# Hybrid decoder layer in three FFN passes: what stands between two passes, and the order of convolution and norm at the mixers' end

## The chip, the cores and the metric

The kernel runs on one core of a Trainium2 chip. The metric is the device time of one execution in microseconds (us); smaller is better. TensorE (PE) does the matmuls and transposes, VectorE (DVE) elementwise work and reductions, ScalarE (ACT) activations and some copies, GpSimd (POOL) a few small powers, and SyncE (SP) issues nearly all DMAs. Each engine runs its own instructions strictly in the order in which they stand in its program; engines wait for one another by semaphores.

## What is computed

One decoder layer and the final norm, for 2048 prompt tokens and 8 x 4 sample tokens, all in float32 (model width 1024, FFN width 2816):

```
xn   = rmsnorm(h) ; proj = xn @ w_in                  # q, f, i, og | ca, cg
o_a  = HGRN2 recurrence on 4 heads, normed, * silu(og)
o_b  = silu(layernorm(conv31(ca * sigmoid(cg))))      # depthwise, 31 taps
h    = h + concat(o_a, o_b) @ w_out                   # h1
xn2  = rmsnorm(h)
h    = h + (silu(xn2 @ w_gate) * (xn2 @ w_up)) @ w_down      # h2
gate = sigmoid(rmsnorm(h) @ w_ple_gate)
h    = h + gate * (p @ w_ple_proj)                    # h3, p: embedding inputs
y    = rmsnorm(h) * g_final
```

## The kernel before

**Precision.** A float32 product is made of three matmuls on a high and a low part of each operand (`mm3`, lines 541 to 544; in the FFN `mm3s`, line 1632): low x high, high x high, high x low. One weight tile pair `wh`, `wl` (128x512 each) serves four steps of the inner dimension, 12 matmuls.

**Order.** Python generators ("threads") yield operations, waits for events and requests for buffers. A list scheduler (`Sched.run`) with its own clocks picks, at build time, the next operation of each engine: the earliest possible start, and between equals the lower `pen` given at `spawn`. For a TensorE operation of a side thread that could not start at once by its clocks, it adds `SIDE` ns to that start, so that matmuls go ahead of it. What it picks is the fixed program order on the chip.

**Stages.** The mixers run over 8 blocks of 256 tokens, the last one with the 32 sample tokens: in-projection, heads, convolution on DVE (line 393, penalties `PCV` 400 and `PCL` 300), layernorm (`bn` lines 942 to 974), out-projection with the residual input `x_in`. Its result h1 is written to DRAM (`h1d`) and also read back from there. Then come three FFN passes t = 0, 1, 2 over 2 x 348, 2 x 348 and 2 x 344 tokens (two halves h). In a pass the gate and up products are made Strassen-like: seven products over 2x2 blocks (A12, A11, S1, S2, S4, S3, A22; `strassen`), each over four steps kp = 0 to 3 of the inner dimension. Weight pairs for passes 1 and 2 are read from `tch`, `tcl` into a ring of nine.

**What stands around the change.** `norm2(t)` makes the FFN's RMS factor `r2[h]` for both halves and then starts `combine(t, kp)` for kp = 0 to 3: it loads four pieces of h1 (DMA, tiles `h` and `f`), scales each by norm gain and r2 (SCALAR_TENSOR_TENSOR, `gn,r`), and makes the seven operands by sums and high/low splits (`x2h`, `x2l`, `xah`, `xal`). Each combine needs five `tmp2` buffers. `residual()` loads h1 into the tiles to which the down-projection adds. `embed(t)` is the per-layer embedding step at the end of a pass; `norm3(t, h)` is its norm, which gives `r3[h]`; its inputs p are loaded by `pin_load` and fire `pin`. `norm4(t, h)` is the final norm: squares on ACT, adds on DVE, then in `rms2` three transposes on TensorE (line 1315), two reductions (lines 1319, 1322), a power on POOL (line 426), three transposes that spread the factor (line 1330), and eight SCALAR_TENSOR_TENSORs (`gn,px`), each followed by `store_y`.

In the kernel before, `norm2(t)` for t > 0 lets the combines begin only after these waits:

```
yield wait(("a", t - 1, last_chunk, CHUNKS[-1] - 1, 1))
for k in range(2):
    for h in HALVES:
        yield wait(("pin", t - 1, k, h))
for h in HALVES:
    yield wait(("r3", t - 1, h))
```

Of the kernel before, what the change touches and what calls it, by code (L numbers as in the profile page):

```python
# [60 lines left out]
NEARA = 80  # L61
NEARD = 40
PSQ = 0
RANK = {"o": -2.0}
FIRST = "ca0 cg0 iv f0 q0 ca1 cg1 f1 q1 ca2 cg2 f2 q2 ca3 cg3 f3 q3 og"

# [29 lines left out]
class Sched:  # L96
# [2 lines left out]


    LAT = 200.0
    SIDE = 1000.0
    OWN = 130.0
    near = dict(pe=0.0, act=NEARA, dve=NEARD, pool=60.0, sp=0.0)

# [82 lines left out]
    def run(self, last=True):  # L188
        self.advance()
        while self.ready:  # L190
            best = {}
            for i, (th, req) in enumerate(self.ready):
                s = self.start(req)
                e = req[1]
                if e == "pe" and th[0].__name__ not in ("lane", "ffn") and s > self.clock[e]:

                    s += self.SIDE
                rank = (th[3] if th[0].__name__ in ("lane", "ffn") else -9.0) if e == "pe" else th[1]
                key = (max(s, self.clock[e] + self.near[e]), rank, th[2])
                if e not in best or key < best[e][0]:  # L200
                    best[e] = (key, s, i)
            _, s, i = min(best.values(), key=lambda x: x[1])
            th, req = self.ready.pop(i)
            _, eng, dur, fn, R, W, nbytes = req
            fn()
            if eng == "sp":
                self.clock["sp"] = s + 60.0
                self.dma = max(self.dma, s) + nbytes / RATE
                end = self.dma + 2000.0
            else:  # L210
                end = s + dur
                self.clock[eng] = end
            for b in R:
                b.r = max(b.r, end)
            for b in W:
                b.w = end
                b.we = eng
            self.runnable.append((th, None))
            self.advance()
        if last and (self.blocked or any(p.waiting for p in self.pools)):  # L220
            said = [f"{th[0].__name__} waits for {ev}" for ev, ths in self.blocked.items() for th in ths]
            said += [f"{th[0].__name__} waits for {n} of {p.name}" for p in self.pools for th, n in p.waiting]
            raise RuntimeError("stuck:\n" + "\n".join(said))
# [19 lines left out]
def trunk(ctx: ExitStack, tc: tile.TileContext, x_in, p_in, s0_in, c0_in, w_in, w_out, w_gu, w_dn,  # L243
# [1021 lines left out]

    def residual():
        for t in PASSES:
            for m in range(KD):
                for h in HALVES:
                    q = yield acq(hres)  # L1270
                    yield from h1_load(t, h, m, q)
                    res[t, m, h] = q
                    S.fire(("hr", t, m, h))
# [10 lines left out]
            sq[k] = q  # L1284
            S.fire(("sq", tag, k))

    def rms2(n, get):

        tk = toks(n)
        tag, sq = count[0], {}  # L1290
        count[0] += 1
        S.spawn(squares2(n, get, sq, tag), PSQ)
        acc = [None, None]
        for i in range(KD):
            yield wait(("sq", tag, i))
            if i < 2:
                acc[i] = sq[i]
                continue
            a, q = acc[i % 2], sq[i]
            if i == 2:  # L1300
                yield stt(a.ap[:, 0:n], a.ap[:, 0:n], EPS / 128, q.ap[:, 0:n], ALU.add, ALU.add, R=[a, q], W=[a], n=n)
            else:
                yield tt(a.ap[:, 0:n], a.ap[:, 0:n], q.ap[:, 0:n], ALU.add, R=[a, q], W=[a], n=n)
            S.release(tmp2, q)
        a, q = acc
        yield tt(a.ap[:, 0:n], a.ap[:, 0:n], q.ap[:, 0:n], ALU.add, R=[a, q], W=[a], n=n)
        S.release(tmp2, q)
        ss = yield acq(small)
        tn = tk[-1][1]
        yield op("dve", 80.0, lambda: nc.vector.memset(ss.ap[:, 2:3], 1.0), [], [ss])  # L1310
        bank = yield acq(misc)

        def fn():
            for j, (t, w) in enumerate(tk):
                nc.tensor.transpose(bank.ap[0:w, j * 128:(j + 1) * 128], a.ap[:, t:t + w], idn)

        yield op("pe", 100.0 * len(tk), fn, R=[a], W=[bank])
        S.release(tmp2, a)
        yield op("dve", d_tt(256), lambda: nc.vector.tensor_reduce(
            out=ss.ap[:, 0:2], in_=bank.ap[:, 0:256].rearrange("p (j f) -> p j f", j=2),  # L1320
            axis=mybir.AxisListType.X, op=ALU.add), [bank], [ss])
        yield op("dve", d_tt(128), lambda: nc.vector.tensor_reduce(  # L1322
            out=ss.ap[0:tn, 2:3], in_=bank.ap[0:tn, 256:384], axis=mybir.AxisListType.X, op=ALU.add), [bank], [ss])
        S.release(misc, bank)
        yield inverse_root(ss, 128, 0, 8, 3)
        bank = yield acq(misc)

        def fn():
            for j, (t, w) in enumerate(tk):
                nc.tensor.transpose(bank.ap[:, t:t + w], ss.ap[0:w, 8 + j:9 + j].to_broadcast([w, 128]), idn[0:w, 0:w])  # L1330

        yield op("pe", 100.0 * len(tk), fn, R=[ss], W=[bank])
        S.release(small, ss)
        return bank
# [7 lines left out]
    def norm2(t):  # L1342
        if t:
            yield wait(("a", t - 1, 2, 1, 1))
        for h in HALVES:
            def get(k, h=h):
                q = yield acq(tmp2)
                yield from h1_load(t, h, k, q)
                return q, q

            yield from row(HALF[t], get, r2[h], ("r2", t, h))
        if t:
            yield wait(("a", t - 1, last_chunk, CHUNKS[-1] - 1, 1))
            for k in range(2):
                for h in HALVES:
                    yield wait(("pin", t - 1, k, h))
            for h in HALVES:
                yield wait(("r3", t - 1, h))
        else:
            yield wait(("indone", NBLK - 2))  # L1360
            yield wait(("indone", NBLK - 1))
        for kp in range(KP):
            if t == 0 and kp == 2:
                yield wait("ffn")
            if t and kp:

                yield wait(("x2", t, kp - 1, "S3"))
            five = yield acq(tmp2, 5)
            S.spawn(combine(t, kp, five), 350 if t == 0 and kp < 2 else 150 if t else 0)

    def combine(t, kp, five):
        n = HALF[t]
# [51 lines left out]
    S.spawn(lane(1), 30)  # L1424
    S.spawn(load_states(), 0)
    S.spawn(free_tmp2(), 0)
    S.spawn(norm2(0), 350)
    manual = tc.manual_schedule()
    manual.__enter__()
    S.run(False)  # L1430
# [528 lines left out]

    def norm4(t, h):  # L1960
        n = HALF[t]
        bank = yield from rms2(n, of_res(t, h, "h3"))
        for m in range(KD):
            r = res[t, m, h]
            ra = r.ap[:, 0:n]
            yield stt(ra, ra, gn[:, 3, m:m + 1], bank.ap[:, 0:n], ALU.mult, ALU.mult, R=[r, bank], W=[r], n=n)
            S.spawn(store_y(t, h, m), 0)
        S.release(misc, bank)
# [132 lines left out]
```

## Time and profile before

| | us |
|---|---|
| runs | 2639.54, 2645.95, 2644.22 (median 2644.22) |
| profiled execution | 2645.72 |
| its span in the trace | 2644.0 |
| TensorE busy | 2525.0 (96%) |
| VectorE busy | 1978.4 (75%) |
| ScalarE busy | 1082.1 (41%) |
| mean granted TensorE clock | 0.98 of full |

TensorE is busy nearly all the time, so what is to be gained or lost is mostly in the few stretches where it is not. Between neighbouring matmuls of 348 columns the starts lie 0.16 us apart at full clock and 0.29 us at the lower level; a matmul is listed with 0.32 or 0.49 us, since neighbours overlap in the pipeline. In a row of the timeline, the bracket at the end gives the idle time of the engine before that row and what ended it.

### The profile page before, as it was taken

The numbers are of one execution on the slowest core, as the hardware profiler recorded it, in microseconds if no ns is written. First come the engines' busy times: TensorE is split into PE (matmuls) and PEld (weight loads), VectorE is DVE, ScalarE is ACT, GpSimd is POOL, SyncE is SP. The second block draws the span as 40 slices with busy tenths as digits, with TensorE's granted clock in tenths as the row PEclk, the third lists the DMA queues.
The fourth block names the chain that finished last, engine by engine and source line by source line (L and its number), as shares of the span: only waits on it lengthen the run. The fifth ranks groups of instructions, "written<-read, shape, count | busy, mean of one in ns | idle before, by whom it ended". The sixth has DMA issues, their size and how long they took to land.

```text
span 2644.0 us, 44170 instructions
## 1 busy us (share of the span) xinstructions
PE 2525.0 (96%) x15646; PEld 2368.0 (90%) x15646; DVE 1978.4 (75%) x4578; ACT 1082.1 (41%) x2477; POOL 140.4 (5%) x286
## 2 busy tenths in 40 slices
PE   7999999999999799999999899999998799999988
PEld 6987977778887699999999889999998799999977
DVE  8998899679886876666677857686587666677686
ACT  5553344334332343444354433343344334333353
POOL 0111010010110100000000000000000000000010
PEclk9999999999999799999999999999999899999999
DMA  8665646554546684565452374445622555554433
GB/s 310 222 211 187 236 159 199 197 179 162 165 139 204 201 278 164 187 211 177 159 207 74 128 255 169 154 161 192 216 81 96 163 193 195 196 173 162 148 95 118
DMA packets 290510, 470.86 MB, mean 178 GB/s; under 512 B 46576, under 2 KB 88048, under 8 KB 290288
## 3 DMA queue, kind: packets, MB, share of 16 engines
q1 hardware_dynamic: 287984, 466.63, 52.7%
q8 instruction: 123, 2.02, 0.3%
q10 hardware_dynamic: 2304, 1.41, 0.2%
q14 instruction: 99, 0.81, 0.1%
HBM read 368.27 MB, written 99.64 MB: 177 GB/s over the span
## 4 chain that ended last, share of the span: by engine, by line
PE 87%; DVE 6%; DMA 3%; POOL 1%; ACT 1%; issue 1%; SPq 0%; POOLq 0%; DVEq 0%; ACTq 0%
PE pm L1632 27%; PE px L1632 13%; PE pm L542 11%; PE pm L544 11%; PE pm L543 11%; PE px L544 2%; PE px L542 2%; PE px L543 2%; DVE h L390 1%; DVE wl L390 1%; PE pm L610 1%; PE pm L612 1%; PE pm L611 1%; DVE h L393 1%; POOL sm L426 1%
## 5 line engine op out<-in xcount | busy, mean ns | idle before, releaser
L390 DVE TENSOR_TENSOR wl<-raw,wh 128x512 fp32r<-128x512 f32 (+1 forms) x496 | 328.8, 667 | 151.8 <-ACT wh L385 138.9
L385 ACT ACTIVATE wh<-raw 128x512 fp32r<-128x512 f32 (+1 forms) x496 | 295.9, 608 | 309.4 <-PE pm L543 96.5
L542 PE MATMUL pm<-xal,wh 128*128 128x256 f32 (+2 forms) x960 | 324.0, 337 | 8.8 <-DVE xal L390 4.6
L544 PE MATMUL pm<-xah,wl 128*128 128x256 f32 (+2 forms) x960 | 311.1, 324 | 0.9 <-DMA wl<-wcl 0.9
L543 PE MATMUL pm<-xah,wh 128*128 128x256 f32 (+2 forms) x960 | 310.9, 324 | 0.0
L542 PE MATMUL pm<-xol,wh 128*128 128x348 f32 (+4 forms) x751 | 250.7, 334 | 9.2 <-ACT wh L385 5.2
L544 PE MATMUL pm<-xoh,wl 128*128 128x348 f32 (+4 forms) x751 | 246.4, 328 | 0.6 <-DVE wl L390 0.5
L543 PE MATMUL pm<-xoh,wh 128*128 128x348 f32 (+4 forms) x751 | 246.1, 328 | 0.0
L390 DVE TENSOR_TENSOR h<-pm,h 128x348 f32<-128x348 f32 (+1 forms) x335 | 172.5, 517 | 91.5 <-PE pm L544 42.6
L1632 PE MATMUL pm<-xal,wh 128*128 128x348 f32 (+1 forms) x707 | 228.6, 323 | 4.1 <-DVE h L390 1.8
L1632 PE MATMUL pm<-xah,wh 128*128 128x348 f32 (+1 forms) x707 | 227.6, 322 | 0.0
L1632 PE MATMUL pm<-xah,wl 128*128 128x348 f32 (+1 forms) x707 | 227.4, 322 | 0.1
L542 PEld LDWEIGHTS pm<-xal,wh 128*128 128x128 f32 x960 | 183.1, 191 | 36.0 <-issue 8.6
L393 DVE SCALAR_TENSOR_TENSOR t<-u,cvw,t 128x256 f32<-128x256 f32 x448 | 214.0, 478 | 0.0
L544 PEld LDWEIGHTS pm<-xah,wl 128*128 128x128 f32 x960 | 182.3, 190 | 15.8 <-DMA wl<-wcl 1.8
L385 ACT ACTIVATE wh<-tw 128x512 fp32r<-128x512 f32 x146 | 92.0, 630 | 249.7 <-DVE tw L390 92.9
L543 PEld LDWEIGHTS pm<-xah,wh 128*128 128x128 f32 x960 | 183.0, 191 | 11.7
L1632 PE MATMUL pm<-x2l,wh 128*128 128x348 f32 (+1 forms) x533 | 171.5, 322 | 6.1 <-DVE x2l L390 6.1
L426 POOL TENSOR_TENSOR sm<-sm,mhalf 128x2 f32<-128x2 f32 (+3 forms) x79 | 75.1, 952 | 1851.7 <-DVE sm L1322 1736.7
L393 DVE SCALAR_TENSOR_TENSOR h<-u,cvw,h 128x256 f32<-128x256 f32 x360 | 171.1, 476 | 2.2 <-ACT h L385 2.1
L1632 PE MATMUL pm<-x2h,wh 128*128 128x348 f32 (+1 forms) x533 | 171.7, 322 | 0.0
L1632 PE MATMUL pm<-x2h,wl 128*128 128x348 f32 (+1 forms) x533 | 171.7, 322 | 0.0
(292 smaller groups left out, 6513.7 us busy)
## 6 DMA issues: line engine op xcount, KB each, us to landing
raw<-w_gu SPq DMA_DIRECT2D x220, 256.0 KB, 3.2
wh<-wch SPq DMA_DIRECT2D x192, 256.0 KB, 2.8
wl<-wcl SPq DMA_DIRECT2D x192, 256.0 KB, 3.2
wh<-tch SPq DMA_DIRECT2D x176, 256.0 KB, 4.6
wl<-tcl SPq DMA_DIRECT2D x176, 256.0 KB, 4.8
raw<-w_dn SPq DMA_DIRECT2D x132, 256.0 KB, 3.2
tch<-wh SPq DMA_DIRECT2D x88, 256.0 KB, 2.8
tcl<-wl SPq DMA_DIRECT2D x88, 256.0 KB, 2.9
```

What stands on the lines that cost most here:

```text
L385: nc.scalar.activation(out, in_, func, scale=scale, bias=bias, **kw)
L390: return op("dve", d_tt(n), lambda: nc.vector.tensor_tensor(out=out, in0=a, in1=b, op=o), R, W)
L393: return op("dve", d_tt(n, not isinstance(s, float)), lambda: nc.vector.scalar_tensor_tensor(out=out, in0=a, scalar=s, in1=b, op0=o0, op1= ...
L426: return op("pool", 700.0, lambda: nc.gpsimd.tensor_tensor(out=s.ap[0:rows, out:out + n], in0=s.ap[0:rows, lo:lo + n], in1=mhalf[0:rows, 0 ...
L542: nc.tensor.matmul(out, lhsT=wh, rhs=xl, start=first, stop=False)
L543: nc.tensor.matmul(out, lhsT=wh, rhs=xh, start=False, stop=False)
L544: nc.tensor.matmul(out, lhsT=wl, rhs=xh, start=False, stop=last)
L610: nc.tensor.matmul(bank.ap, lhsT=xs[0], rhs=wl, start=(k == 0), stop=False)
L611: nc.tensor.matmul(bank.ap, lhsT=xs[0], rhs=wh, start=False, stop=False)
L612: nc.tensor.matmul(bank.ap, lhsT=xs[1], rhs=wh, start=False, stop=(k == KD - 1))
L1632: nc.tensor.matmul(out, lhsT=a, rhs=b, start=first and i == 0, stop=last and i == 2, skip_group_check=True)
```

## The change

- `PN20` = 900 is the penalty of `norm2(0)` and of `combine(0, kp < 2)`, which was 350: on DVE the convolution (400 and 300) now comes before them where both could start.
- `SIDE` is 4000 ns for threads of norm2, norm3 and norm4 and stays 1000 for the others.
- `residual` for t > 0 waits until product A11 of chunk 0, j = 1 of its own pass has been issued (`zp`).
- `norm4` of passes 0 and 1 waits, before its first transposes, until product A11 of chunk 0, j = h of the next pass has been issued. In the last pass it does not.
- `norm2(t > 0)` starts the combines without waiting for `r3` of the pass before.

```diff
+PN20 = 900
-    SIDE = 1000.0
+    SIDE = dict(norm2=4000.0, norm3=4000.0, norm4=4000.0)
...
-                    s += self.SIDE
+                    s += self.SIDE.get(th[0].__name__, 1000.0)
...
     def residual():
         for t in PASSES:
+            if t:
+                yield wait(("zp", t, 0, 1, 1))
...
-    def rms2(n, get):
+    def rms2(n, get, late=None):
...
+        if late:
+            yield wait(late)
         bank = yield acq(misc)
...
                     yield wait(("pin", t - 1, k, h))
-            for h in HALVES:
-                yield wait(("r3", t - 1, h))
...
-            S.spawn(combine(t, kp, five), 350 if t == 0 and kp < 2 else 150 if t else 0)
+            S.spawn(combine(t, kp, five), PN20 if t == 0 and kp < 2 else 150 if t else 0)
...
-    S.spawn(norm2(0), 350)
+    S.spawn(norm2(0), PN20)
...
-        bank = yield from rms2(n, of_res(t, h, "h3"))
+        bank = yield from rms2(n, of_res(t, h, "h3"), None if t == PASSES[-1] else ("zp", t + 1, 0, h, 1))
```

**Place 1, TensorE between pass 0 and pass 1.** Before, the last matmuls of A12's steps kp 0 to 2 (operands `xal`, `xah`) are followed by the twelve transposes of both halves' final norm, and only then by step kp 3 (`x2l`, `x2h`). Line 1315 is the first set of transposes, line 1330 the second:

```order
L1632 MATMUL px_181<-xah,wl_81 128x348
L1315 MATMUL px_179<-idn,f_9125 128x128 x2
L1315 MATMUL px_179<-idn,f_9125 92x128
L1315 MATMUL px_182<-idn,f_9123 128x128 x2
L1315 MATMUL px_182<-idn,f_9123 92x128
L1330 MATMUL px_179<-idn,sm_67 128x128 x2
L1330 MATMUL px_179<-idn,sm_67 128x92
L1330 MATMUL px_182<-idn,sm_71 128x128 x2
L1330 MATMUL px_182<-idn,sm_71 128x92
L1632 MATMUL px_181<-x2l,wh_80 128x348
L1632 MATMUL px_181<-x2h,wh_80 128x348
```

In the changed kernel (its line numbers are 1 to 5 higher: 1632 is 1635, 1315 is 1320, 1330 is 1335) kp 3 follows at once, then A11:

```order
L1635 MATMUL px_180<-xah,wl_81 128x348
L1635 MATMUL px_180<-x2l,wh_80 128x348
L1635 MATMUL px_180<-x2h,wh_80 128x348
L1635 MATMUL px_180<-x2h,wl_81 128x348
L1635 MATMUL pm_176<-xal,wh_84 128x348
L1635 MATMUL pm_176<-xah,wh_84 128x348
```

The first half's transposes of line 1320 now come 24 matmul rows after these, behind S1, and its line 1335 another 24 matmuls behind that; the second half's follow 46 rows later with 18 matmuls between them.

**Place 2, DVE between pass 1 and pass 2.** The last operand before TensorE can do kp 3 of A12 is the `x2l` of `f`. Line 1319 and 1322 are the final norm's reductions, `gn,px` its last step, `gn,r` the combine's scaling. Before:

```order
L390 TENSOR_TENSOR h_77<-h_77 128x344
L1310 MEMSET sm_73 128x1
L1319 TENSOR_REDUCE sm_72<-px_179 128x2
L1319 TENSOR_REDUCE sm_73<-px_182 128x2
L1322 TENSOR_REDUCE sm_72<-px_179 92x1
L1322 TENSOR_REDUCE sm_73<-px_182 92x1
L393 SCALAR_TENSOR_TENSOR h_77<-h_77,gn,r_115 128x344
L393 SCALAR_TENSOR_TENSOR f_9124<-f_9124,gn,r_115 128x344
L390 TENSOR_TENSOR x2l<-f_9124,x2h 128x344
L390 TENSOR_TENSOR x2l<-h_77,x2h 128x344
L393 SCALAR_TENSOR_TENSOR h_76<-h_76,gn,px_179 128x348 x2
```

And in the changed kernel:

```order
L391 TENSOR_TENSOR f_9126<-f_9126,f_9123 128x348
L391 TENSOR_TENSOR f_9127<-f_9127,f_9126 128x348
L1313 MEMSET sm_73 128x1
L394 SCALAR_TENSOR_TENSOR h_77<-h_77,gn,r_115 128x344
L394 SCALAR_TENSOR_TENSOR f_9124<-f_9124,gn,r_115 128x344
L391 TENSOR_TENSOR x2l<-f_9124,x2h 128x344
L391 TENSOR_TENSOR x2l<-h_77,x2h 128x344
L391 TENSOR_TENSOR h_77<-h_77 128x344
L391 TENSOR_TENSOR x2l<-h_77,x2h 128x344 x2
```

The reductions and the final norm's `gn,px` left this place, but the final norm's adds (`f_9126`, `f_9127`) still stand ahead of A12's `x2l`. Behind it the sums of S1, S2 and S4 now follow without `gn,px` between them.

**Place 3, TensorE at the mixers' end.** Line 942 and 974 are the layernorm's transposes in and out, `px<-idn,h_77` with line 1315 and 1330 is `norm2(0)` of the second half (its first half stands earlier), and line 542 with `xol` starts the last out-projection. Before:

```order
L942 MATMUL px_181<-idn,h_78 32x128 x4
L1205 MATMUL px_179<-idn,t_155 128x128 x2
L1207 MATMUL px_179<-idn,t_153 128x32
L1315 MATMUL px_179<-idn,h_77 128x128 x2
L1315 MATMUL px_179<-idn,h_77 92x128
L1330 MATMUL px_180<-idn,sm_69 128x128 x2
L1330 MATMUL px_180<-idn,sm_69 128x92
L974 MATMUL px_179<-idn,h_78 128x128 x2
...
L974 MATMUL px_181<-idn,u_149 128x32
L542 MATMUL pm_177<-xol,wh_96 128x256
```

And in the changed kernel:

```order
L1320 MATMUL px_180<-idn,h_77 128x128 x2
L1320 MATMUL px_180<-idn,h_77 92x128
L1335 MATMUL px_179<-idn,sm_69 128x128 x2
L1335 MATMUL px_179<-idn,sm_69 128x92
L975 MATMUL px_182<-idn,h_78 128x128 x2
...
L975 MATMUL px_179<-idn,u_149 128x32
L1320 MATMUL px_182<-idn,h_77 128x128 x2
L1320 MATMUL px_182<-idn,h_77 92x128
L1335 MATMUL px_180<-idn,sm_74 128x128 x2
L1335 MATMUL px_180<-idn,sm_74 128x92
L543 MATMUL pm_177<-xol,wh_96 128x256
```

Both halves of `norm2(0)` moved back by about one half: the first now stands ahead of the layernorm's transposes out, and the second is the last thing ahead of the out-projection. On DVE eleven of `norm2(0)`'s adds moved from before to behind the end of the convolution.

On SP, `x_in` of the last block now goes ahead of all eight loads of combine kp 0 and 1 (before, kp 0's four went first). Between passes the y stores and the residual loads stand among the weight loads of the next pass. In the changed order the longest run of SP entries without a weight load from `tch` is 21 y stores, between pass 1 and 2.

## Rows read from the trace of the kernel before

**Rows 1.** The page: busy time, share of the span, instructions.

```profile
PE 2525.0 (96%) x15646; PEld 2368.0 (90%) x15646; DVE 1978.4 (75%) x4578; ACT 1082.1 (41%) x2477; POOL 140.4 (5%) x286
```

**Rows 2.** Stretches: length; PE, PEld, DVE, ACT, POOL busy (count); clock; DMA share; GB/s.

```profile
850.00:900.00 50.00, 37.11 (x231) 29.38 (x229) 42.19 (x134) 16.89 (x46) 7.82 (x15) 0.81 0.63 194
...
1450.00:1500.00 50.00, 50.00 (x316) 50.00 (x315) 42.12 (x87) 23.32 (x50) 0.00 (x0) 1.00 0.31 102
1500.00:1550.00 50.00, 34.06 (x198) 32.15 (x197) 31.86 (x69) 15.02 (x32) 1.67 (x2) 0.83 0.73 222
...
2050.00:2100.00 50.00, 36.44 (x199) 34.68 (x199) 38.71 (x83) 16.89 (x36) 2.78 (x2) 0.86 0.47 149
```

**Rows 3.** Timeline of TensorE between pass 0 and 1.

```profile
1511.17 0.99 PE L1315 MATMUL px<-idn,f 128*128 128x128 f32 x6 [3.21 <-DVE sm L1310]
1513.90 1.66 PE L1330 MATMUL px<-idn,sm 128*128 128x128 f32 x6 [1.74 <-POOL sm L426]
1526.18 0.66 PE L1632 MATMUL px<-x2l,wh 128*128 128x348 f32 x1 [10.62 <-DVE x2l L390]
...
1529.19 0.32 PE L1632 MATMUL pm<-xah,wh 128*128 128x348 f32 x1
```

**Rows 4.** Timeline of VectorE there, first and last combine.

```profile
1442.68 0.58 DVE L393 SCALAR_TENSOR_TENSOR h<-h,gn,r 128x348 f32<-128x348 f32 x1
...
1494.34 0.52 DVE L390 TENSOR_TENSOR pm<-pm,r 128x348 f32<-128x348 f32 x1
...
1517.81 6.42 DVE L393 SCALAR_TENSOR_TENSOR h<-h,gn,px 128x348 f32<-128x348 f32 x13
...
1525.61 0.52 DVE L390 TENSOR_TENSOR x2l<-f,x2h 128x348 fp32r<-128x348 f32 x1
```

**Rows 5.** Timeline of TensorE between pass 1 and 2.

```profile
2073.87 0.32 PE L1632 MATMUL pm<-xah,wl 128*128 128x344 f32 x1
2078.70 0.90 PE L1315 MATMUL px<-idn,f 128*128 128x128 f32 x3 [4.51 <-DVE sm L1310]
...
2096.78 0.66 PE L1632 MATMUL pm<-x2l,wh 128*128 128x344 f32 x1 [6.06 <-DVE x2l L390]
...
2103.78 0.31 PE L1632 MATMUL px<-xal,wh 128*128 128x344 f32 x1
...
2119.55 0.55 PE L1632 MATMUL px<-xal,wh 128*128 128x344 f32 x1 [2.44 <-DMA wh<-tch]
```

**Rows 6.** Timeline of VectorE there.

```profile
2079.20 0.52 DVE L390 TENSOR_TENSOR h<-h 128x348 f32<-128x348 f32 x1
...
2081.45 0.56 DVE L393 SCALAR_TENSOR_TENSOR h<-h,gn,r 128x344 f32<-128x344 f32 x1
...
2083.06 0.52 DVE L390 TENSOR_TENSOR x2l<-f,x2h 128x344 fp32r<-128x344 f32 x1 [0.56 <-ACT x2h L385]
...
2090.28 4.96 DVE L393 SCALAR_TENSOR_TENSOR h<-h,gn,px 128x348 f32<-128x348 f32 x10
```

**Rows 7.** Timeline of SP's queue there.

```profile
2086.73 5.69 SPq L471 DMA_DIRECT2D y<-h  x12
```

**Rows 8.** Timeline of POOL: two powers of one norm.

```profile
1985.17 5.48 POOL L426 TENSOR_TENSOR sm<-sm,mhalf 128x3 f32<-128x3 f32 x1 [192.69 <-DVE sm L1322]
2001.94 0.85 POOL L426 TENSOR_TENSOR sm<-sm,mhalf 128x3 f32<-128x3 f32 x1 [11.29 <-DVE sm L1322]
```

**Rows 9.** Timeline of TensorE and VectorE at the mixers' end.

```profile
902.68 0.58 PE L542 MATMUL pm<-xol,wh 128*128 128x256 f32 x1
...
923.92 0.39 PE L542 MATMUL pm<-xol,wh 128*128 128x256 f32 x1 [4.04 <-DVE h L390]
...
888.63 0.19 DVE L390 TENSOR_TENSOR h<-h,t 128x32 f32<-128x32 f32 x1
...
898.78 0.58 DVE L393 SCALAR_TENSOR_TENSOR h<-h,gn,r 128x348 f32<-128x348 f32 x1 [0.61 <-ACT r L385]
...
923.45 0.75 DVE L390 TENSOR_TENSOR h<-h,pm 128x256 f32<-128x256 f32 x2
```

## What I predict for the changed kernel

> **What bounds the kernel now.** I read the page first: TensorE is busy for 2525.0 of 2644 us and DVE for three quarters [rows 1], so time can only come from stretches in which TensorE is not at full rate. Next the busy time in stretches of 50 us. A full stretch holds 316 matmuls at clock 1.00, one every 0.158 us; three stand far below it: 231 at the mixers' end (850 to 900), 198 between pass 0 and 1, 199 between pass 1 and 2 [rows 2]. Then the timelines of TensorE and of its releasers in these three places, where the change acts.
>
> *Between pass 0 and 1* the last matmul of A12's kp 0 to 2 is listed until 1507.96 (3.21 before 1511.17); its successor could have started 0.16 earlier, since neighbours overlap by half, at 1507.80. The next 348-column ones come at 1526.18, at the lower clock until just before 1529.19 [rows 3]. In order: 3.21 us of wait for the final norm's sums, transposes, then 10.62 for `x2l` of kp 3. On DVE that `x2l` (1525.61) stood behind the final norm's `gn,px` of 6.42 us and four more of them, and the first combine had only begun at 1442.68 [rows 4]. From 1507.80 to 1529.19 are 21.4 us; the 10 matmuls in it are worth 1.6 and the twelve transposes about 1.8 at full clock (an estimate: 0.15 each), so 18.0 are lost.
>
> *Between pass 1 and 2* there are a wait of 4.51 before the transposes, one of 6.06 for the `x2l` of S1, and low clock until just before 2103.78; from 2074.03 that is 29.75 us with 53 matmuls (8.4) and the same transposes: 19.6 lost. A weight tile is late by 2.44 at 2119.55 [rows 5]; with the low clock after it (the 10 matmuls at 1526.18 took 3.0 in place of 1.6, so 1.4 more [rows 3]) 3.8. Together 23.4.
>
> *At the mixers' end* the last convolution operation is at 888.63, the out-projection starts at 902.68, runs out of banks, and goes on at 923.92, released by the first bank evacuation, which stands on DVE at 923.45 behind combine kp 0 and 1; these began at 898.78 [rows 9].
>
> **The change, part by part.**
>
> *The combines of pass 1 don't wait for r3.* They need r2, the pins and buffers, all there early. By the new order kp 3's `x2l` stands just behind a gate evacuation that the trace has at 1494.34 [rows 4]; TensorE wants it at 1507.8 [rows 3], 13 us later. kp 3 doesn't wait any more, unless DVE slips by 13 us.
>
> *Final norm's transposes behind A11 of the next pass.* TensorE runs from A12 into A11 and S1, and meets the transposes when their inputs are long there. Between the first and the second set stand 24 or 18 matmuls, 3.8 or 2.8 us; the reductions and the power between them took 1.74 before, the wait listed at 1513.90 [rows 3]. They fit if DVE takes the reductions up at once; I put 1.5 us for waits that are left at this place. The eight `gn,px` of a half are still DVE work, but no operand of the next products stands behind them. **Term: 18.0 - 1.5 = 16.5 gained.** Bounds: 18 (no wait), 13 (two waits of about 2.5).
>
> *The same between pass 1 and 2.* Here the new order still has A12's `x2l` behind the final norm's adds. The last add starts at 2079.20; before, reductions lay between it and the combine's scaling at 2081.45, and the `x2l` pair began 1.6 us behind that [rows 6]. Without the reductions the scaling starts at 2079.7 and `x2l` is done 2.1 us later, at 2081.8. TensorE wants it at 2074.0: a wait of 7.8 stays, with 1.4 of low clock behind it and 1 for the second transposes, 10.2 in all. The 6.06 for S1 go, since the 4.96 of `gn,px` that stood ahead of it on DVE [rows 6] moved behind S1's, S2's and S4's sums. **Term: 23.4 - 10.2 = 13.2 gained.** Bounds: 20 (the adds, which wait for gates, come earlier since the combine's loads do), 6 (S1 or the weights still wait).
>
> *y stores and residual loads among the weight loads.* Twelve y stores took 5.69 us of SP's queue, 0.47 each, whatever their size [rows 7]. Before, all 48 and the 16 residual loads stood nearly in a block, with which the late weight at 2119.55 fits [rows 5]. Now the longest block is 21 stores, 9.9 us. The ring of nine pairs covers 9 x 12 x 0.158 = 17 us, so I take the 3.8 as gained; the residual loads have cover too, since their first user, chunk 0's down-projection, comes more than two j (2 x 84 matmuls, 26 us) after the event they wait for. If the cover is gone it is a bank that DVE can't evacuate. The Trainium skill, page "DMA: Bandwidth & Descriptors", section "Issuing engines are not separate DMA queues", says that the sequencer's time to initiate a DMA is usually small relative to the DMA itself. By that rule the block of stores was no cause, the wait at 2119 stays, and the sum is 3.8 higher; the row, half a microsecond of queue per store, speaks against it here, so the sum goes by the row.
>
> *Convolution first.* Eleven adds of `norm2(0)` at about 0.43 us go behind the convolution's end, which comes up to 4.7 us earlier. But they are not gone: norm2's second half now ends last. I walked DVE's new order with the durations before, an estimate: convolution ends at 883, layernorm's transposes out 894 to 897.5, the last add ends at 903, then transposes, reductions, a power, transposes; the out-projection starts near 907 in place of 902.68. r2 is there at 908; the combines take from 898.78 to 923.45 before, 24.7 us, of which 2.2 were a wait for loads and 1.3 splits that now stand ahead: the first evacuation moves to 929.2, **5.8 us lost** [rows 9]. The banks run out in the same way, so the start of the out-projection hardly matters; the evacuation does. Bounds: a gain of 3 (layernorm earlier, DVE's idle time takes the adds) and a loss of 10: the power of this norm, taken at 0.85, also occurs at 5.48 [rows 8].
>
> *SIDE 4000* moves norm3's transposes in pass 0 by at most 18 matmuls, 2.8 us. Gate matmuls and splits of the other half lie beside it; I take nothing, bounds 0 and 2.8.
>
> **Sum.** 2645.7 (the profiled time; span 2644.0) - 16.5 - 13.2 + 5.8 = 2621.8. The median of the runs is 1.5 below the profiled time, so 2621 is what I say.
>
> **Rivals.**
>
> *A: the mixers' end is neutral or gains.* For it: DVE was busy for 42 of the 50 us to 900 [rows 2], so 8 us of idle could take the eleven adds. Against: combine needs r2 of both halves, and the last add is now behind the layernorm. With 0 to 3 gained: 2613 to 2616.
>
> *B: new waits in the next pass.* A second set of transposes waits for a power of 5.48 in place of 0.85 [rows 8], 4.6 us more than the 1.74 above, 6.4 against a cover of 2.8 to 3.8: about 3 us each, four times, 12 us: 2633. For it: TensorE takes its rows in order, and the reductions stand on a DVE that is now busier with the combine there. Against: the long power came after 192.69 us of idle POOL, and one with 11.29 before it took 0.85.
>
> *C: the stores hold the weights, slower.* Place: SP's queue at the start of passes 1 and 2. A y store that stands early waits there for its `gn,px`, and every weight load behind it too. With pins holding four of the nine ring places the cover is 5 x 1.9 = 9.5 us, no more than the block of 21 stores; each further microsecond that DVE lags goes onto TensorE. It decides from 12 us of lag at each boundary, 24 together; ten `gn,px` take DVE 4.96 [rows 6], a pass's sixteen about 8, so such a lag needs more than all of them to stand in front. Price with 16 each: 2654. The page named above, section "Anatomy of one DMA", has the wait for a semaphore on the issuing sequencer, not on the DMA engine, which is this mechanism; no row of before shows a weight held for that reason.
>
> *D: the gain is not there.* TensorE, ahead by 16 us, runs into buffers of `embed` or `hid` that DVE frees at its old pace, since DVE's work is unchanged. Against: DVE is idle for a quarter of the time [rows 1]. It would give half the gains back: about 2637.
>
> **Chances.** Forecast 0.53 (2614 to 2630 by its own terms), A 0.20, B 0.14, D 0.07, C 0.06. The range runs from the sum of the best bounds that I hold likely (-18, -18, -3: 2607) to B with a bad mixers' end, 2637; it leaves out C and part of D. About 0.3%, 8 us, is what a measurement can tell here: faster by that (below 2636) 0.85, within it 0.09, slower 0.06.
>
> **What would show it.** In the changed profile: no wait for `x2l` of 10 us near 1500 and over 300 matmuls in that stretch; between pass 1 and 2 one wait for `x2l` of A12 near 8 us and none for S1; no wait for weights 45 us behind it; the out-projection's bank wait later by about 6 us relative to the end of the in-projections, and the second half's transposes right ahead of it. The forecast is wrong if transposes of lines 1320 or 1335 wait for more than 2 us inside the next pass, if weights from `tch` wait there, or if the first evacuation at the mixers' end is not later.

## The result, and the profile after

| | before | changed |
|---|---|---|
| median of the runs | 2645.01 | 2624.68 |
| lowest and highest | 2639.54, 2645.95 | 2622.25, 2628.81 |
| profiled execution, its span | 2645.72, 2644.0 | 2628.81, 2627.1 |

The medians differ by 20.3 us. The ratio of the runs is 0.9929, 95% interval 0.991 to 0.9948, which is 0.7% faster. 2621 was forecast, with 2607 to 2637. Two terms of the sum were nevertheless well off, and they are what this section and the runs are about.

The busy time by stretch, columns as in [rows 2], shows where the time came from and where it stayed. The first row is the kernel before, the others are the changed kernel:

```profile
900.00:950.00 50.00, 45.96 (x325) 44.47 (x326) 35.87 (x79) 16.78 (x38) 0.00 (x0) 0.89 0.67 223
```

```profile
850.00:900.00 50.00, 36.94 (x231) 28.58 (x230) 39.17 (x124) 16.23 (x46) 5.90 (x13) 0.83 0.57 171
900.00:950.00 50.00, 35.07 (x245) 34.44 (x246) 31.78 (x72) 13.63 (x32) 0.85 (x1) 0.79 0.65 218
1500.00:1550.00 50.00, 50.00 (x321) 49.92 (x320) 38.63 (x83) 21.47 (x45) 1.70 (x2) 1.00 0.74 239
2050.00:2100.00 50.00, 37.74 (x227) 37.03 (x226) 33.44 (x72) 16.69 (x35) 1.81 (x2) 0.90 0.52 163
2100.00:2150.00 50.00, 47.17 (x286) 45.95 (x285) 31.24 (x66) 19.29 (x41) 0.00 (x0) 0.97 0.78 266
```

The hole between pass 0 and 1 is gone (321 matmuls in place of 198), the one between pass 1 and 2 is not (227 in place of 199), and the one from 900 to 950 has grown (245 in place of 325).

To see each stage by itself I took, from TensorE's timeline of each kernel, the start of the same product matmul and subtracted its start in the kernel before. In us, negative is earlier:

| start of | before at | changed |
|---|---|---|
| first product of the FFN | 959.30 | +9.6 |
| A12 of pass 1 | 1506.36 | +8.9 |
| the 400th product matmul behind it | 1590.74 | -8.7 |
| A12 of pass 2 | 2072.62 | -10.9 |
| the 400th behind it | 2161.34 | -15.0 |
| last product matmul | 2540.57 | -15.1 |
| last transposes | 2635.40 | -16.9 |

So the mixers' end lost 9.6 (forecast 5.8), the first boundary (the stretch between pass 0 and 1, from A12 to the 400th product) gained 17.7 (16.5), the second, between pass 1 and 2, 4.1 (13.2), and the ends of pass 1 and 2 gained 2.2 and 1.8, of which I had forecast nothing. The trace's sum is 16.9 and the median's 20.3; the profiled execution is the longest of the four. Single us of these lines are not to be trusted: FFN starts of one order differ by some us from trace to trace (below), and two runs below whose instructions stand in the same order at the second boundary gained 5.8 and 6.0 there.

TensorE's waits over 0.8 us in the changed kernel from the mixers' end to the second boundary:

```profile
895.27 0.84 PE L1335 MATMUL px<-idn,sm 128*128 128x128 f32 x3 [4.41 <-POOL sm L427]
904.27 0.87 PE L1320 MATMUL px<-idn,h 128*128 128x128 f32 x3 [4.91 <-DVE sm L1313]
906.79 0.84 PE L1335 MATMUL px<-idn,sm 128*128 128x128 f32 x3 [1.65 <-POOL sm L427]
932.69 0.58 PE L543 MATMUL pm<-xol,wh 128*128 128x256 f32 x1 [9.01 <-DVE h L391]
1561.80 0.42 PE L1635 MATMUL pm<-xal,wh 128*128 128x348 f32 x1 [1.15 <-DMA wh<-tch]
1983.37 0.84 PE L1335 MATMUL px<-idn,sm 128*128 128x128 f32 x3 [7.39 <-POOL sm L427]
2072.83 0.65 PE L1635 MATMUL pm<-x2l,wh 128*128 128x344 f32 x1 [9.52 <-DVE x2l L391]
2086.37 0.43 PE L1635 MATMUL pm<-x2l,wh 128*128 128x344 f32 x1 [2.74 <-DVE x2l L391]
2124.90 0.42 PE L1635 MATMUL px<-xal,wh 128*128 128x344 f32 x1 [2.65 <-DMA wh<-tch]
```

The reader is to see three things. The final norm's transposes (lines 1320 and 1335 near 1520 and 2080) are not in this list: inside the next pass they wait for nothing. The bank wait of the out-projection went from 4.04 [rows 9] to 9.01. And at the second boundary A12's wait is 9.52, the weights' 2.65 in place of 2.44 [rows 5], and S1's 6.06 is gone, but a wait of 2.74 stands at kp 3 of S4. (A product has twelve matmuls; counted from A12's first, without the transposes, the wait at 2086.37 is in the fifth product, which is S4, and that at 2096.78 before is in the third, S1.)

VectorE's rows ahead of that wait of 9.52 say what was late:

```profile
2066.92 1.07 DVE L391 TENSOR_TENSOR f<-f,f 128x348 f32<-128x348 f32 x2
2070.05 0.58 DVE L394 SCALAR_TENSOR_TENSOR h<-h,gn,r 128x344 f32<-128x344 f32 x1 [2.05 <-DMA h<-h1d]
2071.12 0.58 DVE L394 SCALAR_TENSOR_TENSOR f<-f,gn,r 128x344 f32<-128x344 f32 x1 [0.49 <-DMA f<-h1d]
2072.25 0.52 DVE L391 TENSOR_TENSOR x2l<-f,x2h 128x344 fp32r<-128x344 f32 x1 [0.56 <-ACT x2h L386]
...
2082.39 3.50 DVE L394 SCALAR_TENSOR_TENSOR h<-h,gn,px 128x348 f32<-128x348 f32 x7
```

The norm's adds were done at 2068, about where I had put them, but then VectorE waited for combine kp 3's own loads. They had been issued late; SP's timeline:

```profile
2064.82 0.42 SPq L472 DMA_DIRECT2D h<-h1d  x1
2065.47 0.33 SPq L472 DMA_DIRECT2D raw<-w_gu  x1
2065.85 0.48 SPq L472 DMA_DIRECT2D f<-h1d  x1
...
2084.73 11.60 SPq L472 DMA_DIRECT2D y<-h  x21
```

And eight of the final norm's `gn,px` (seven of them the 3.50 us at 2082.39) stand ahead of an operand on VectorE: the low part of S4. S4's sum comes before them, but its `x2l` only behind them, at 2085.80.

### The profile page after: what moved, and what is told of

It reads as the page before. It is cut to its first block, busy times and chain, and to the rows that moved or that the text cites. A ratio compares the mean times of both kernels' runs of the same rounds, so it can differ in the third digit from the quotient of the medians.

```text
span 2627.1 us, 44191 instructions
## 1 busy us (share of the span) xinstructions
PE 2514.9 (96%) x15646; PEld 2361.8 (90%) x15646; DVE 1975.2 (75%) x4578; ACT 1080.8 (41%) x2477; POOL 141.4 (5%) x286
## 4 chain that ended last, share of the span: by engine, by line
PE 88%; DVE 5%; DMA 3%; ACT 2%; POOL 2%; issue 1%; SPq 0%; POOLq 0%; DVEq 0%; ACTq 0%
PE pm L1635 27%; PE px L1635 13%; PE pm L543 11%; PE pm L545 11%; PE pm L544 11%; PE px L545 2%; PE px L543 2%; PE px L544 2%; DVE h L391 1%; PE pm L611 1%; PE pm L613 1%; PE pm L612 1%; POOL sm L427 1%; DVE wl L391 1%; PE px L1135 1%; PE px L1102 1%
```

## The experiments

All ratios are to the kernel before, on the same chip. The changed kernel has 0.9929 [0.991, 0.9948].

**The mixers' order back.**

```diff
-PN20 = 900
+PN20 = 350
```

> The changed kernel with PN20 back at 350, all else as changed. Theory 1 (the convolution-first order at the mixers' end costs what the trace of the changed kernel shows, 9.6 us up to the FFN's first product, and nothing later depends on it): the FFN starts about 9.6 us earlier, the bank wait of the out-projection is about 4 us again in place of 9.0, and the time falls by 8 to 11 us, to about 2615. Rival (the passes only gain because the combines of pass 0 and the convolution stand in the new order; the gains of the later places shrink with it): the time stays within 3 us of the changed kernel, 2625. If the order was a help at the mixers' end, the time rises.

0.9901 [0.9884, 0.9918], about 7 us better than the changed kernel. Its FFN starts at +2.1, and the order of the passes is that of the changed kernel (18.9 and 5.8 gained at the two boundaries). TensorE's bank wait fell less than expected:

```profile
898.43 0.84 PE L1335 MATMUL px<-idn,sm 128*128 128x128 f32 x3 [6.17 <-POOL sm L427]
...
925.75 0.58 PE L543 MATMUL pm<-xol,wh 128*128 128x256 f32 x1 [7.17 <-DVE h L391]
```

Here the out-projection starts as early as before (-0.2), but the first evacuation still comes 1.8 later than in [rows 9]. Over all traces of this study the FFN starts at +5.2 to +10.8 with PN20 at 900 (eight traces, mean 9.2) and at 0 to +4.5 with 350 (six, mean 2.5): convolution first costs 6.7 us.

**Transposes of the final norm at once.**

```diff
-rms2(n, of_res(t, h, "h3"), None if t == PASSES[-1] else ("zp", t + 1, 0, h, 1))
+rms2(n, of_res(t, h, "h3"), None)
```

> The changed kernel, but the final norm of passes 0 and 1 no longer waits for the next pass before its transposes. Theory 1 (between pass 0 and 1 the gain comes from the combines that no longer wait for r3; between pass 1 and 2 the later transposes bring little, since A12's last operand is late anyhow): the first boundary keeps its 18 us to within 3, the second loses at most its 4 us, time 2625 to 2630. Rival (the later transposes carry the gain): the waits of 3.2 and 4.5 us before the transposes and of 6 to 10 us behind the final norm's scaling come back, time 2638 to 2645.

0.9957 [0.9942, 0.9972]: 7 us lost, a little more than expected. The first boundary keeps 15.5 of 17.7, the second loses all of its 4.1. The waits at the second are like those of before: 4.15 for the sums, 3.70 and 5.00 for `x2l`, 3.52 for weights.

**The combines wait for r3 again.**

```diff
+            for h in HALVES:
+                yield wait(("r3", t - 1, h))
```

> The changed kernel, but the combines of passes 1 and 2 wait for r3 of the pass before again; the transposes stay late. Theory 1: between pass 0 and 1 kp 3 of A12 is late again, by 8 to 10 us and not by 21 since the final norm's scaling no longer stands ahead of it; so about half of the 18 us is lost there, little between pass 1 and 2, time 2632 to 2637. Rival (the later transposes carry the gain): the time stays near 2625. Rival 2 (r3 carries all of it): 2643.

0.9992 [0.9982, 1.0003]. I had expected half of the first boundary's gain to stay; 2.7 us of 17.7 did. TensorE and VectorE there:

```profile
1525.22 0.58 DVE L394 SCALAR_TENSOR_TENSOR f<-f,gn,r 128x348 f32<-128x348 f32 x1 [2.99 <-DMA f<-h1d]
...
1528.83 0.66 PE L1637 MATMUL px<-x2l,wh 128*128 128x348 f32 x1 [10.64 <-DVE x2l L391]
1541.40 0.43 PE L1637 MATMUL pm<-x2l,wh 128*128 128x348 f32 x1 [2.69 <-DVE x2l L391]
```

The wait for `x2l` is as long as before (10.62 [rows 3]). The transposes, and with them 5 us of waiting, left this place, but TensorE only arrives earlier at kp 3, whose loads are late by themselves, and the final norm's `gn,px` then hold S4. With the combines late, moving the transposes only changes the name of the wait there. The second boundary kept its gain (6.8), where the run above, without the later transposes, had 0.1: there it is the transposes that count.

**One part alone: r3's wait removed from the kernel before.**

```diff
-            for h in HALVES:
-                yield wait(("r3", t - 1, h))
```

> The kernel before with one part alone: the combines of passes 1 and 2 no longer wait for r3. Theory 2 (after the run that put that wait back: this part carries nearly all of the gain between pass 0 and 1, and the order of the mixers' end is a loss): boundary 0 to 1 gains 17 to 19 us, boundary 1 to 2 0 to 3, the mixers' end stays, time 0.992 to 0.994 of the kernel before, as much as the whole change. Rival (it needs the later transposes and the later residual loads with it): less than 10 us gained, 0.997.

0.9952 [0.9937, 0.9967], less than expected and more than the rival. The first boundary gains 15.1, the second 1.7. So this part carries most of the first boundary and little of the second. The later transposes add 2.2 at the first and 4 at the second by the run above, 7 us in all by its time.

**y stores from POOL.**

```diff
-            if t == PASSES[-1] and m % 2:
+            if t != PASSES[-1]:
+                yield op("pool", 60.0, lambda d=dst, s=src: nc.gpsimd.dma_start(out=d, in_=s), [r])
+            elif m % 2:
```

> The changed kernel with the y stores of passes 0 and 1 issued by POOL in place of SP. Theory 1 (SP's queue, half a microsecond per y store, makes the weights late at the start of passes 1 and 2, 1.15 us at 1561.8 and 2.65 us at 2124.9 with low clock behind it): both waits go, the time falls by 4 to 6 us, to about 2620. Rival (the DMA engines or the ring of nine weight pairs are what is short there): the waits stay, time within 2 us of 2625. A third outcome: POOL takes longer per store than SP, stores end later and hold the residual tiles, time above 2625.

0.9912 [0.9899, 0.9926]. No row waits for `tch` any more at the start of a pass, and the stretch in which the wait of 2.65 stood is full:

```profile
2100.00:2150.00 50.00, 50.00 (x320) 49.80 (x319) 35.80 (x76) 21.11 (x45) 8.41 (x16) 1.00 0.70 240
```

320 matmuls at clock 1.00 against 286 at 0.97 in the changed kernel. The second boundary gains 9.8, that is 5.7 more than in the changed kernel's trace, and the first 1.3 more. TensorE's and VectorE's orders are the same in both, so the stores' place in SP's queue was the cause. The size is less sure than the cause: in the run with PN20 350 and in the one with SIDE 1000 (below), with the stores on SP and the same order at this place, the weights' wait was 1.21 and 1.35 in place of 2.65 and the boundary gained 5.8 and 6.0, so the stores cost some 4 to 6 us there.

**Residual loads early again.**

```diff
-            if t:
-                yield wait(("zp", t, 0, 1, 1))
```

> The changed kernel with the residual loads of passes 1 and 2 as early as before; only SP's order differs. Theory: they fall into the same stretch as the y stores either way, so the weights are late by 1 to 5 us more at the start of passes 1 and 2, time 0 to 5 us above the changed kernel. Rival (loading them later buys nothing): within 1.5 us.

0.9941 [0.9926, 0.9955], an interval that overlaps with the changed kernel's, 3 us above it in the middle. In the trace the first boundary gains 2.1 less (weights are 1.76 late there, 1.15 in the changed kernel) and the second 1.6 less, no more than traces of one order differ there. Loading them later may be worth some 3 us; that is not shown.

**SIDE back to 1000.**

```diff
-    SIDE = dict(norm2=4000.0, norm3=4000.0, norm4=4000.0)
+    SIDE = dict()
```

> The changed kernel with SIDE at 1000 for all threads again. TensorE's and SP's orders are then the same as in the changed kernel, VectorE's differs in about ten rows. Theory: SIDE 4000 brings nothing once the other parts are there; time within 2 us of the changed kernel. Rival: the few rows matter where the waits are; more than 3 us.

0.9941 [0.992, 0.9963]: unclear in the times, but the traces speak against the theory. The ends of pass 1 and 2 lose 0.7 and 2.8 us; at the end of pass 1 TensorE waits 5.67 for a power and then 2.59 for a high part, as before, in place of 7.39 alone. The end of pass 2 bears this out in all traces: from the last product to the last transposes the eleven kernels with SIDE 4000 gain 0.7 to 1.8 on the kernel before, the two others with 1000 lose 0.9 and 1.0. What differs in the order at the end of pass 1 is no row of VectorE (its ten rows are at the mixers' end), but one copy of r on ACT, which stands ahead of the high parts.

**Final norm late from its squares on.** The same wait, at the head of `rms2`:

```diff
     def rms2(n, get, late=None):
+        if late:
+            yield wait(late)
...
-        if late:
-            yield wait(late)
         bank = yield acq(misc)
```

> The changed kernel, but the final norm of passes 0 and 1 waits for the next pass before its squares, not only before its transposes. Theory 3 (the 9.5 us that A12's last operand is late between pass 1 and 2 come from the final norm's squares: they hold tmp2 buffers that the combine's loads need, and their adds stand ahead on VectorE): the wait at 2072.8 goes, 8 to 12 us gained there, time 2613 to 2618. Rival (the loads are late because SP's queue holds them behind raw weights): A12's operand stays late by 6 us or more. A further risk: the residual tiles come free later, and the y stores and residual loads make weights or the down-projection late, which takes some of it back.

0.9896 [0.9881, 0.991]. The second boundary gains 16.7 in place of 4.1. kp 3's loads are issued at 2049.66 in place of 2064.82 (this kernel's pass ends 2.4 us earlier), and its `x2l` is done at 2057.8, before TensorE begins A12 at 2059.3. SP's and VectorE's timelines:

```profile
2049.66 3.18 SPq L472 DMA_DIRECT2D f<-h1d  x4
...
2055.27 1.06 DVE L394 SCALAR_TENSOR_TENSOR f<-f,gn,r 128x344 f32<-128x344 f32 x2 [0.81 <-DMA f<-h1d]
2056.89 0.95 DVE L391 TENSOR_TENSOR x2l<-f,x2h 128x344 fp32r<-128x344 f32 x2 [0.56 <-ACT x2h L386]
```

The four loads stand together in the queue now, and all four tiles are `f`. What remains at TensorE is 3.03 for a later `x2l` (2069.53) and 0.90 for weights.

**The combines' loads from POOL.** To part the causes, only the loads' queue is changed. The last argument makes `h1_load` use `nc.gpsimd.dma_start`, and the scheduler reckons with POOL's loads as with SP's:

```diff
-            yield from h1_load(t, h, k, q)
+            yield from h1_load(t, h, k, q, t > 0)
```

> The changed kernel with the combines' loads of h1 in passes 1 and 2 issued by POOL in place of SP, so that no raw weight stands ahead of them in a queue. Theory 3 (tmp2 buffers, held by the final norm's squares, and their adds on VectorE keep A12's last operand late between pass 1 and 2): the wait of 9.5 us stays above 7. Rival (SP's queue held the loads): it falls below 5 us, as it did to 3.0 with the squares late.

0.9918 [0.9899, 0.9937]. A12 waits 6.64, between the two:

```profile
2068.47 0.66 PE L1638 MATMUL pm<-x2l,wh 128*128 128x344 f32 x1 [6.64 <-DVE x2l L391]
```

So SP's queue (raw weights that wait for VectorE stood ahead of the loads) held about 3 of the 9.5 us; the rest goes only when the squares and adds go. The rows of this run part the rest:

```profile
2058.09 0.54 POOL L1264 DMA_DIRECT2D f<-h1d  x1
...
2065.28 1.07 DVE L391 TENSOR_TENSOR f<-f,f 128x348 f32<-128x348 f32 x2
2066.28 0.57 DVE L394 SCALAR_TENSOR_TENSOR h<-h,gn,r 128x344 f32<-128x344 f32 x1
```

The last load of kp 3 is issued at 2058.09, and none of the four took more than 4.6 us to land, so the data was there by 2062.7. The scaling ran at 2066.28 without a wait for a load, behind the norm's adds and other VectorE work. By these rows, an estimate, VectorE's order held 3.6 us of the 6.64, and some 3 are left for loads that could be issued only late.

**The three together.** PN20 350, y stores from POOL, the wait at the head of `rms2`.

> All three together on the changed kernel: PN20 350, y stores of passes 0 and 1 issued by POOL, final norm late from its squares on. If the parts add up (8 from the mixers' end, 5 from the stores, 8 to 12 from the squares): 21 to 25 us below the changed kernel, 0.984 of the kernel before. If the stores and the squares save the same wait: 14 to 18 us, 0.987.

0.987 [0.9853, 0.9886], 2608.72 against 2644.08 on that chip: faster than both kernels. By the ratio it is 16 us below the changed kernel, as if stores and squares saved in part the same. The waits do not show that: with the squares alone the weights' waits at the second boundary were 0.90 and 0.69, against 1.21 to 2.65 in the traces with the changed kernel's order. The boundaries gain 19.0 and 19.5, no weight is waited for in the passes, and at the second boundary 3.00 for an `x2l` and 1.71 for a power are left.

**An extra power ahead of norm3's.** In the last version, for h = 0 of passes 1 and 2; its result is used nowhere:

```diff
+            yield wait(("h2", t, 3, h))
+            s0 = yield acq(small)
+            yield op("dve", 80.0, lambda: nc.vector.memset(s0.ap[:, 0:3], 1.0), [], [s0])
+            yield inverse_root(s0, 128, 0, 8, 3)
+            S.release(small, s0)
         yield from row(HALF[t], of_res(t, h, "h2"), r3[h], ("r3", t, h))
```

> The best version so far (PN20 350, y stores on POOL, final norm late from its squares on) with one more power on POOL, of ones, a few microseconds ahead of norm3's first power in passes 1 and 2; its result is not used. If the 5 to 7 us of that power in every run come from its being the first on POOL in a long time or after some instruction it has to fetch, the extra power takes them off the path: the waits of 7.4 us before the second transposes fall to about 3, 4 to 5 us gained twice, time 8 to 11 us below the best version. If they belong to the power's own numbers or to the traffic at that place, the waits stay and the time is within 2 us of it.

0.9863 [0.9842, 0.9884], no change. POOL's idle time before the power fell to 20 us, its length did not move:

```profile
1967.97 7.21 POOL L427 TENSOR_TENSOR sm<-sm,mhalf 128x3 f32<-128x3 f32 x1 [20.26 <-DVE sm L1327]
```

**VectorE stands still for the power.**

In norm3 of passes 1 and 2 (`late` is set to "dve" there):

```diff
         yield inverse_root(ss, 128, 0, 8, 3)
+        if late == "dve":
+            yield op("dve", 80.0, lambda: nc.vector.tensor_copy(ss.ap[:, 12:13], ss.ap[:, 8:9]), [ss], [ss])
```

> The best version (as in the run with all three, without the extra power), with one small copy on VectorE behind norm3's power in passes 1 and 2, so that VectorE stands still until POOL has done the power. Theory 4 (POOL's power of 5 to 7 us is not slow, it is held while VectorE runs operations back to back there, and ends in VectorE's first gap): VectorE reaches the copy some 1.5 us after the reductions, the power ends within 1 us behind that, so it takes 2 to 3 us in place of 7.2, and TensorE's wait before the second transposes falls to about 3; the time hardly moves, since TensorE needs VectorE's splits next, 2605 to 2612. Rival (the power itself takes 7 us there): VectorE waits for it for over 5 us, the power stays at 7 and the time rises by 8 us or more.

0.988 [0.9863, 0.9897]. The power takes 2.04, and ends as VectorE waits for it:

```profile
1969.20 2.04 POOL L427 TENSOR_TENSOR sm<-sm,mhalf 128x3 f32<-128x3 f32 x1 [192.68 <-DVE sm L1327]
...
1969.96 0.57 DVE L394 SCALAR_TENSOR_TENSOR hxl<-h,gn,hxh 128x348 fp32r<-128x348 f32 x1
1971.27 0.15 DVE L1332 COPY sm<-sm 128x1 f32<-128x1 f32 x1 [0.74 <-POOL sm L427]
```

TensorE's wait for it falls from 7.37 to 2.21, and 1.96 for a high part and 2.96 for a low part take its place. VectorE's splits are the bound there, not the power.

## Why the prediction held, and where it did not

*Between pass 0 and 1* the mechanism and the size were right: 17.7 for 16.5. kp 3 is ready, and both sets of transposes are hidden. The run with r3's wait back and the one with it alone removed agree that the freed combines carry most of it. (Sixteen `gn,px` stood ahead of kp 3's `x2l` before, three more than the row's 13 and not four, which changes nothing.)

*Between pass 1 and 2* the step that failed is "a wait of 7.8 stays, with 1.4 of low clock behind it and 1 for the second transposes, 10.2 in all". The term was mis-sized, 13.2 for 4.1 in this trace (5.8 and 6.0 in two others of the same order), in three pieces. First, A12's wait was 9.52: I let the scaling start when VectorE was free, and took the loads to be there; they came 2.05 later. Second, S1's wait did go, as I had put it, but I looked only at the sums of S1, S2 and S4: S4's `x2l` stands behind eight `gn,px`, and its kp 3 waited 2.74. Third, the weights' wait, taken as gained with its low clock, 3.8 in all, stayed. The runs showed the real owner of the first piece: the final norm's squares and adds ran before the wait that holds its transposes, so they still took tmp2 buffers and VectorE's time ahead of the combine (16.7 gained with the wait ahead of them; 7.7 with another queue for the loads alone). By the rows of that last run, SP's queue, VectorE's order and the late issue of the loads held about 3 us each, an estimate; that buffers were what made the loads late is argued from the code and not measured by itself.

*y stores.* The row's half microsecond per store was the right measure; my conclusion from it was not. I set the longest block, 21 stores and 9.9 us, against a full ring of 17 and found cover. The block took 11.60, but it is not one block that counts. From 2081.9 to 2119.8 SP issued all 40 y stores of the pass (not 48, as I had it), nine loads of h1 and only six weight pairs; the seventh, issued at 2119.87, is the one that TensorE waited for at 2124.90. At a pair per 1.9 us TensorE could have used twenty in that time. And SP itself waits for VectorE's `gn,px` in front of stores. SP's waits from 2080 to 2125 (us in total, times, longest):

```profile
SPq L472 <- DVE h L394: 4.2, 3, 3.8
```

The run with the stores on POOL settles it: no weight wait is left. The rule of the Trainium skill that I weighed against the row, that the sequencer's time to initiate a DMA is usually small relative to the DMA itself ("DMA: Bandwidth & Descriptors", "Issuing engines are not separate DMA queues"), gave the right time for that one piece (the wait stayed) for the wrong reason. Here the 21 stores held the queue for 11.60 us, and moving them to POOL removed the wait.

*The mixers' end.* Direction and mechanism were right, the size 5.8 for 6.7 over all traces (9.6 in this one). The first evacuation stands at 932.2, for 929.2. The 2.2 us that I took off for kp 1's loads did not go: its scaling waits for loads of h1 again, 0.98, 0.55 and 1.15. And kp 0 starts at 909.9 though r2 is there at 908.1, as I had put it: its own loads, which SP issues from 904.62 on, right behind `x_in`, are late. The first row is kp 0's scaling, the second the last of kp 1's:

```profile
909.89 2.06 DVE L394 SCALAR_TENSOR_TENSOR h<-h,gn,r 128x348 f32<-128x348 f32 x4 [4.09 <-DMA h<-h1d]
...
923.77 0.58 DVE L394 SCALAR_TENSOR_TENSOR h<-h,gn,r 128x348 f32<-128x348 f32 x1 [1.15 <-DMA h<-h1d]
```

*SIDE*, which I put at nothing, gave 3.5 us by two traces, at the ends of pass 1 and 2, where I had not looked.

*The sum.* In the trace of the changed kernel the second boundary gained 9.1 less than I had put down and the mixers' end cost 3.8 more. Both make the time longer. The first boundary, the ends of pass 1 and 2 and the rest gave back 5.9, of which I had forecast nothing. So the trace is 7.0 short of the 23.9 forecast, and the medians, with 20.3, are 3.6 short. That the time came out closer than its terms is in part luck. (2621.8 less 1.5 is 2620.3, which I rounded up to 2621.)

*The rivals.* A (mixers' end neutral) is refuted by the run with PN20 350, B (new waits at the second transposes) by their absence from the waits, D by the full stretches behind the first boundary. C's place and cause were real (SP's wait of 4.2 us above), but the wait for weights was about the one that was there before, 2.65 for 2.44, not a loss of 16.

## What to carry to other kernels

- When a step is moved behind a wait, look at all that it does ahead of that wait: here the squares and adds in front kept the loads and the engine's time, 10 us and more, and the transposes behind it were the cheap part, 4 to 6 us at that place.
- A wait that goes shows the next one in line. Before striking it out, check that the next operand's loads, buffers and queue place are early too; the second boundary had three such waits behind one another.
- Count stores in the issuing queue by their number, not their bytes, and over the whole stretch, not by the longest block. Give them a queue with nothing behind it.

## What the runs showed of the hardware

In the second half of the kernel a power on POOL of 128x3 elements took 0.85 us in most places and 5.4 to 7.2 in norm3 of passes 1 and 2 (spans on POOL are rough, but TensorE's wait for the power moves with them). It is not a matter of POOL having been idle: 7.18 after 192 us of idle time in the changed kernel, 7.21 after 20, and 0.85 after 246.94 elsewhere in the kernel before. It follows VectorE. In the changed kernel VectorE runs without a gap from 1975 to 1983, from the power's start to 1982.53 with two inputs in SBUF each time, and the power ends only when an operation with an operand in PSUM (`px`) comes; with SIDE 1000 it ends at 1982.23, 0.7 us after VectorE's gap of 2.52 before 1984.04 begins:

```profile
1976.13 7.18 POOL L427 TENSOR_TENSOR sm<-sm,mhalf 128x3 f32<-128x3 f32 x1 [192.65 <-DVE sm L1327]
...
1981.67 0.94 DVE L391 TENSOR_TENSOR wl<-f,wh 128x348 fp32r<-128x348 f32 x2
1982.53 0.51 DVE L391 TENSOR_TENSOR h<-px,h 128x348 f32<-128x348 f32 x1
```

```profile
1976.75 5.48 POOL L427 TENSOR_TENSOR sm<-sm,mhalf 128x3 f32<-128x3 f32 x1 [192.63 <-DVE sm L1327]
...
1984.04 0.95 DVE L391 TENSOR_TENSOR wl<-h,wh 128x348 fp32r<-128x348 f32 x2 [2.52 <-ACT wh L386]
```

Making VectorE wait for it cut it to 2.04, and there too it ended 0.7 us after VectorE fell idle. The Trainium skill, page "GPSIMD Engine Reference", section "1. Specifications", says that POOL's interfaces to SBUF are shared with VectorE, with contention from VectorE instructions that are in a 2-port mode or have two SBUF inputs. The traces agree, and the run with the pause shows by intervention that VectorE's work is what holds the power; that the SBUF interfaces are the way in which it does is the page's account, and no run here shows it. In rival B I had taken the long power as a matter of POOL's idle time; that was wrong.
